# Hybrid attention and PEER layer: head-group norms in two parts, value columns moved behind the last latent head, second LayerNorm by token halves with float32 products

## The chip, the cores and the metric

The kernel runs on one core of one Trainium2 chip. The metric is device time in microseconds of one execution. The core has TensorE (PE, matmuls), VectorE (DVE), ScalarE (ACT), GpSimd (POOL, unused here) and SyncE (SP), on whose queue every DMA of this kernel is issued.

## The reference

One decoder layer on 256 tokens of width 2048, all in float32. `x` and `c` are inputs, `mod = silu(c) @ w_ada + b_ada` gives six vectors of 2048 (shift, scale and gate of the two sub-layers).

```
h   = LN0(x) * (1 + sc1) + sh1
proj = h @ w_in                       # 8 heads' q, k, v (3 x 1024), two latents of 512, a 64-wide key
o_a = dilated window attention, 8 heads of 128         # group A
o_b = latent attention (w_uq, w_uk, w_uv), 8 heads     # group B
o   = concat(rms_norm(o_a) * g_a, rms_norm(o_b) * g_b)  # each over 1024 columns
x1  = LN(alpha * x + g1 * (o @ w_o)) * ln1_g + ln1_b
h2  = LN0(x1) * (1 + sc2) + sh2
q   = h2 @ w_pq                       # scores against two key sets, top 16, softmax: gates
out = LN(alpha * x1 + g2 * (gelu(h2 @ u.T) * gates) @ v) * ln2_g + ln2_b
```

The norms need the whole row: the mean square of the 1024 columns of a head group, and mean and variance of 2048 columns.

## The kernel before

The 256 tokens stand as two halves (`th`) of 128 partitions. Activations that feed a matmul are transposed to columns: 16 chunks of 128 features by 256 tokens. Most matmuls are made in three products of a rounded part and a remainder (`mm3`, L139: hi x hi, hi x lo, lo x hi, type fp32r): `piece` (L94) loads 1 MB of weights as 4 x 512 columns, ACT rounds it to `hi` (L101), DVE takes the remainder `lo` (L103), two halves each, from rings of three `raw`, four `hi` and four `lo` buffers. Some pieces are multiplied in plain float32 (L150, L157, L334), which takes two instructions per matmul in the trace.

The stages, in order of time: w_in in four k groups (0 to about 250 us), with the products of the last group between the first heads; heads of group A 0 to 3 and of group B 0 to 7 (to 333); the norms and the last four heads of A; w_o in 16 pieces (348 to 452); the two LayerNorms in a row (`affine`, L695); w_pq in four k groups (472 to 575); the u table with the search for the top 16 (to 1320); the v table and the last LayerNorm.

Beside all of it runs the product with w_ada: `ada` (L207) loads one block of 1 MB, and DVE multiplies and sums it in two halves (L212) into one column of `modc`. 32 blocks belong to the first k groups; the other 48 (16 of the gate g1, 32 of shift and scale of the second sub-layer, in the order of the k groups that need them) come from a generator, `ada_rest` (L244), and `ada_pull(n)` (L259) asks for the next n. `PULLS`, `PULL_WO` and `PULL_PQ` say how many at which place. They go through two buffers, so that a block's load waits until DVE is done with the block two before.

A planner orders the work: it takes the instructions in the order in which the program makes them as priorities, simulates the engines, and fixes one order for each engine and for the DMA queue, in which they then run; an instruction that waits holds up all behind it on its engine. `tc.issue_after(ins)` puts the instructions of its block that are on the engine of `ins` behind it in that order.

The places that the change touches: `attend` (L415) is one head's softmax and its product with the values; a head of A reads its values from `proj` columns 2048 to 3071, which are the pieces n = 4 and 5 of w_in, the heads 4 to 7 of them piece 5 (L580). `row_norm` (L458) squares a group's 1024 columns on ACT (L462), makes the reciprocal root in small steps on DVE (`rstd_of`, L166) and scales the columns; `to_operand` (L488) transposes them (L481), scales by the gain (L485) and splits. In the program's order, the norm of B stands before heads 4 and 5 of A, and the norm of A behind the w_o pieces of steps 0 to 3, whose operands come from B alone. `spread_cols` (L229) makes the row of the gate g1 in all partitions: 16 diagonals on DVE (L235), 16 float32 matmuls against ones (L236). In `affine`, the residual's norm is applied in four pieces of 512 columns (L701, L702), with statistics of the result (L703) for the second norm (`norm_of`, L687); `to_xT` (L709) normalises, transposes (L716) and, for the first 512 columns, modulates and splits. Both halves have to be there before the first w_pq piece, since its products are 256 tokens wide.

## Time and profile before

| | us |
|---|---|
| median of 3 runs | 2043.37 (2042.28 to 2044.26) |
| profiled execution | 2044.22 |
| its span, first to last instruction | 2042.4 |
| TensorE busy | 1973.8 (97%) |
| VectorE busy | 1497.3 (73%) |
| ScalarE busy | 1048.2 (51%) |
| DMA, mean share of 16 engines | 73.5% |

A row of a timeline gives the start in us from the span's first instruction, the duration, engine, line, operation, what it writes and reads, and, in brackets, how long its engine had stood idle and what ended that. PEclk is the granted share of TensorE's full clock (2.4 GHz); it has two levels, 1.0 and 0.5. A matmul's duration holds its latency, so the distance between starts is the price of one in a row of them.

### The profile page before, as it was taken

The numbers are of one execution on the slowest core, as the hardware profiler recorded it, in microseconds if no ns is written. First come the engines' busy times: TensorE is split into PE (matmuls) and PEld (weight loads), VectorE is DVE, ScalarE is ACT, GpSimd is POOL, SyncE is SP. The second block draws the span as 40 slices with busy tenths as digits, with TensorE's granted clock in tenths as the row PEclk, the third lists the DMA queues.
The fourth block names the chain that finished last, engine by engine and source line by source line (L and its number), as shares of the span: only waits on it lengthen the run. The fifth ranks groups of instructions, "written<-read, shape, count | busy, mean of one in ns | idle before, by whom it ended". The sixth has DMA issues, their size and how long they took to land.

```text
span 2042.4 us, 26235 instructions
## 1 busy us (share of the span) xinstructions
PE 1973.8 (97%) x10072; PEld 1644.3 (81%) x10072; DVE 1497.3 (73%) x2344; ACT 1048.2 (51%) x1538; POOL 0.2 (0%) x4
## 2 busy tenths in 40 slices
PE   6999998988999999999999999999999999999997
PEld 4567686778998888888888888888888788888886
DVE  7588987889799868677777766686776666554557
ACT  2333457435444665677777775444444444444451
POOL 0000000000000000000000000000000000000000
PEclk7999998998999999999999999999999999999999
DMA  8887887867646566667777668989999988765552
GB/s 349 338 332 304 314 324 268 331 267 277 241 147 215 219 239 254 235 255 273 270 287 265 266 238 308 316 337 324 329 337 324 304 290 286 278 227 202 189 207 102
DMA packets 142830, 554.82 MB, mean 272 GB/s; under 512 B 10864, under 2 KB 77552, under 8 KB 84848
## 3 DMA queue, kind: packets, MB, share of 16 engines
q1 hardware_dynamic: 142704, 553.14, 73.5%
q8 instruction: 79, 1.29, 0.2%
q14 instruction: 47, 0.39, 0.1%
HBM read 502.76 MB, written 50.34 MB: 271 GB/s over the span
## 4 chain that ended last, share of the span: by engine, by line
PE 85%; DVE 9%; DMA 3%; ACT 2%; issue 1%; SPq 0%; DVEq 0%; ACTq 0%
PE u_ps L135 21%; PE u_ps L136 11%; PE v_ps L141 10%; PE v_ps L140 10%; PE v_ps L142 10%; PE win_ps L334 3%; DVE ada L212 2%; PE win_ps L141 2%; DMA gl<-g_d 2%; PE win_ps L142 2%; PE g_ps L942 2%; PE win_ps L140 1%; PE wo_ps L142 1%; PE wo_ps L141 1%; PE wo_ps L140 1%
## 5 line engine op out<-in xcount | busy, mean ns | idle before, releaser
L135 PE MATMUL u_ps<-act,hi_u 128*128 128x512 f32 x2048 | 721.6, 396 | 0.0
L136 PE MATMUL u_ps<-act,lo_u 128*128 128x256 f32 x2048 | 575.1, 281 | 0.9 <-DVE lo_u L103 0.9
L135 PEld LDWEIGHTS u_ps<-act,hi_u 128*128 128x128 f32 x2048 | 384.5, 188 | 87.7
L101 ACT CAST hi_v<-raw_v 128x1024 fp32r<-128x1024 f32 x244 | 256.8, 1054 | 332.0 <-PE v_ps L142 298.6
L103 DVE TENSOR_TENSOR lo_v<-raw_v,hi_v 128x1024 fp32r<-128x1024 f32 x244 | 295.6, 1222 | 173.0 <-ACT hi_v L101 172.9
L103 DVE TENSOR_TENSOR lo_u<-raw_u,hi_u 128x1024 fp32r<-128x1024 f32 x256 | 312.3, 1221 | 137.7 <-ACT hi_u L101 136.5
L136 PEld LDWEIGHTS u_ps<-act,lo_u 128*128 128x128 f32 x2048 | 386.6, 189 | 3.9 <-DVE lo_u L103 3.7
L141 PE MATMUL v_ps<-lo_v,whi 128*128 128x512 f32 x976 | 380.0, 389 | 2.3 <-DVE lo_v L103 2.3
L140 PE MATMUL v_ps<-hi_v,whi 128*128 128x512 f32 x976 | 379.9, 389 | 1.0 <-DVE W L798 1.0
L142 PE MATMUL v_ps<-hi_v,wlo 128*128 128x512 f32 x976 | 379.7, 389 | 0.0
L101 ACT CAST hi_u<-raw_u 128x1024 fp32r<-128x1024 f32 x256 | 267.3, 1048 | 174.4 <-PE u_ps L135 163.3
L141 PEld LDWEIGHTS v_ps<-lo_v,whi 128*128 128x128 f32 x976 | 183.2, 188 | 41.0 <-DVE lo_v L103 3.5
L140 PEld LDWEIGHTS v_ps<-hi_v,whi 128*128 128x128 f32 x976 | 183.2, 188 | 40.1 <-DVE W L798 1.8
L142 PEld LDWEIGHTS v_ps<-hi_v,wlo 128*128 128x128 f32 x976 | 183.2, 188 | 38.1
L212 DVE SCALAR_TENSOR_TENSOR ada<-ada,cb 128x1024 f32<-128x1024 f32 x160 | 191.0, 1218 | 9.9 <-DMA ada<-in_w_ada_dram 9.8
L937 DVE TENSOR_TENSOR o<-eq,gT 128x1024 fp32r<-128x1024 f32 x64 | 78.3, 1223 | 33.3 <-PE g_ps L942 33.3
L334 PE MATMUL win_ps<-raw_win,hmod 128*128 128x512 f32 x192 | 86.4, 605 | 1.2 <-ACT hmod L305 1.2
L799 ACT ACTIVATE W<-W 128x512 f32<-128x512 f32 x64 | 40.7, 636 | 73.4 <-DVE W L798 73.4
L140 PE MATMUL wpq_ps<-act,hi_wpq 128*128 128x256 f32 x256 | 73.6, 290 | 2.3 <-ACT act L160 2.1
L142 PE MATMUL wpq_ps<-act,lo_wpq 128*128 128x256 f32 x256 | 72.8, 286 | 0.5 <-DVE lo_wpq L103 0.5
L141 PE MATMUL wpq_ps<-act,hi_wpq 128*128 128x256 f32 x256 | 73.0, 286 | 0.0
L101 ACT CAST hi_win<-raw_win 128x1024 fp32r<-128x1024 f32 x40 | 40.9, 1049 | 61.4 <-PE win_ps L142 30.8
(329 smaller groups left out, 2407.1 us busy)
## 6 DMA issues: line engine op xcount, KB each, us to landing
raw_u<-in_u_dram SPq DMA_DIRECT2D x128, 1024.0 KB, 5.3
raw_v<-in_v_dram SPq DMA_DIRECT2D x122, 1024.0 KB, 6.6
ada<-in_w_ada_dram SPq DMA_DIRECT2D x80, 1024.0 KB, 6.9
raw_win<-in_w_in_dram SPq DMA_DIRECT2D x32, 1024.0 KB, 8.9
g_d<-stg SPq DMA_DIRECT2D x16, 2048.0 KB, 7.2
gl<-g_d SPq DMA_DIRECT2D x32, 1024.0 KB, 10.1
raw_wo<-in_w_o_dram SPq DMA_DIRECT2D x16, 1024.0 KB, 6.9
raw_wpq<-in_w_pq_dram SPq DMA_DIRECT2D x16, 1024.0 KB, 6.9
```

The costliest lines, as they stand in the source:

```text
L101: nc.scalar.copy(hi, raw[:, 2 * j:2 * j + 2, :])
L103: nc.vector.tensor_sub(lo, raw[:, 2 * j:2 * j + 2, :], hi.bitcast(F32))
L135: nc.tensor.matmul(pss[e], hi[:, i, es], act[:, k], start=first and j == 0 and i == 0, stop=False)
L136: nc.tensor.matmul(pss[e][:, 1], lo[:, i, es], act_hi[:, k, :], start=False, stop=last and j == 1 and i == 3)
L140: nc.tensor.matmul(o, sh, mh, start=start, stop=False)
L141: nc.tensor.matmul(o, sh, ml, start=False, stop=False)
L142: nc.tensor.matmul(o, sl, mh, start=False, stop=stop)
L212: nc.vector.scalar_tensor_tensor(w[:, z, :], w[:, z, :], 1.0, cb[:, z * 1024:(z + 1) * 1024], op0=ALU.mult, op1=ALU.mult, accum_out=(modc, ...
L334: nc.tensor.matmul(ps[th], act[:, i, ts], src[:, i, :], start=i == 0, stop=i == 3)
L799: nc.scalar.activation(ws, ws, AF.Gelu)
L937: nc.vector.tensor_mul(o2, eq.unsqueeze(2).broadcast_to(both), gT[:, four, :].bitcast(F32).unsqueeze(3).broadcast_to(both))
L942: nc.tensor.matmul(ps[:, q * T:(q + 1) * T], o1[:, 2 * j + q, :], o2[:, 2 * j + q].rearrange("p z n -> p (z n)"), start=True, stop=True)
```

## The change

It does the following. (1) The w_in piece n = 5 of the last k group is made behind head 7 of group B, not before the heads; the scores of heads 4 and 5 of A stand before it. (2) `row_norm` of a head group takes the squares of seven heads early (`early_squares`) and of the eighth at the end; the small steps of the reciprocal root become two fewer. (3) The norm of A and its transposes stand before the w_o pieces in the program's order; the w_ada pulls of steps 0 to 3 are queued behind `norm_done` on DVE. (4) The row of g1 is made from one transpose and one DMA to DRAM as soon as its 16 columns are there, and read back as a broadcast. (5) `affine` works in halves of 1024 columns; the second norm's sums come with the second instruction, its squares from ACT. (6) The w_pq pieces of k group 0 for n = 0, 1, 2 are multiplied in float32, one token half at a time, the first half behind the first half's norm; n = 3 remains a split piece. (7) The pulls are set anew.

```diff
-PULLS = (2, 1, 1, 3, 0, 1, 1, 1, 3, 1, 0, 1)
-PULL_WO = (2, 3, 0, 1, 1, 1, 1, 1, 0, 0, 1, 2)
+PULL_IN = (0, 1, 0)
+PULLS = (2, 1, 1, 3, 0, 1, 1, 1, 3, 1, 0, 0)
+PULL_WO = (0, 1, 1, 1, 1, 1, 1, 1, 1, 1, 1, 2)
...
-        nc.vector.tensor_mul(t, t, ve)
-        nc.vector.tensor_scalar(t, t, -0.5, 1.5, op0=ALU.mult, op1=ALU.add)
-        last_rstd[0] = nc.vector.tensor_mul(r, r, t)
+        nc.vector.scalar_tensor_tensor(t, t, -0.5, ve, op0=ALU.mult, op1=ALU.mult)
+        last_rstd[0] = nc.vector.scalar_tensor_tensor(r, t, 1.5, r, op0=ALU.add, op1=ALU.mult)
...
+    def row_of(col0):
+        ps = bank("tr", f"row_ps{col0}")
         nc.tensor.transpose(ps[:16, :P], modc[:, col0:col0 + 16], ident)
+        rowt = stream.tile([P, 2, 512], F32, tag="lo", name=f"rowt{col0}", bufs=4)[:16, 0, :P]
         nc.scalar.copy(rowt, ps[:16, :P])
         nc.sync.dma_start(row_d.rearrange("(c p) -> c p", p=P), rowt)
...
             ada_bias(G1, 16)
+            row_of(G1)
...
                         ada_in(kg + 1, m)
                         m += 1
+                    ada_pull(PULL_IN[kg])
...
+            def squares(c0, n, ms):
                 for th in range(2):
                     nc.scalar.activation(junk[:, :n], proj[:, th, c0:c0 + n], AF.Square, accum_out=ms[:, th:th + 1])
...
+            def row_norm(c0, n, name, early=None):
+                ms = mix.tile([P, 2], F32, tag="ms", name=f"ms_{name}", bufs=2)
+                if early is None:
+                    squares(c0, n, ms)
+                    nc.vector.tensor_scalar(ms, ms, 1.0 / n, 1e-6, op0=ALU.mult, op1=ALU.add)
+                else:
+                    squares(c0 + n - P, P, ms)
+                    nc.vector.scalar_tensor_tensor(ms, ms, 1.0 / n, early, op0=ALU.mult, op1=ALU.add)
...
+            def early_squares(c0, name):
+                ms = mix.tile([P, 2], F32, tag="mse", name=f"mse_{name}", bufs=1)
+                squares(c0, 1024 - P, ms)
+                nc.vector.tensor_scalar(ms, ms, 1.0 / 1024, 1e-6, op0=ALU.mult, op1=ALU.add)
+                return ms
...
-            for n in (1, 3, 5):
+            for n in (1, 3):
                 w_in_pieces(3, (n,), hmod3)
                 ada_pull(PULLS[2])
...
-            for h in (4, 5, 6, 7):
+            for h in (4, 5, 6):
                 heads_b(h)
                 ada_pull(PULLS[11])
-            row_norm(1024, 1024, "ob")
-            heads_a(2, last_a[0])
+            ms_b = early_squares(1024, "ob")
+            first[3, 5] = piece(a["w_in"][3, 5], "win3_5")
+            heads_b(7)
+            last_s = [scores_a(*last_a[0], h) for h in (4, 5)]
+            with tc.issue_after(last_o[0].ins):
+                w_in_pieces(3, (5,), hmod3)
+            row_norm(1024, 1024, "ob", ms_b)
+            heads_a(2, last_a[0], scores=last_s)
             to_operand(1024, 8, V_GOUT + 8, "ob0")
             to_operand(1536, 12, V_GOUT + 12, "ob1")
-            heads_a(3, last_a[1])
+            heads_a(3, last_a[1], (0,))
+            ms_a = early_squares(0, "oa")
+            heads_a(3, last_a[1], (1,))
+            norm_done = row_norm(0, 1024, "oa", ms_a)
+            to_operand(0, 0, V_GOUT, "oa0")
+            to_operand(512, 4, V_GOUT + 4, "oa1")
             for step in range(4):
                 w_o_piece(step)
-            norm_done = row_norm(0, 1024, "oa")
-            to_operand(0, 0, V_GOUT, "oa0")
-            to_operand(512, 4, V_GOUT + 4, "oa1")
...
-            spread_cols(g1b, modc[:, G1:G1 + KC], "g1")
+            bcast_row(g1b, row_d)
...
                 if step >= 4:
                     w_o_piece(step)
-                ada_pull(PULL_WO[step])
+                    ada_pull(PULL_WO[step])
+                else:
+                    with tc.issue_after(norm_done.ins):
+                        ada_pull(PULL_WO[step])
...
             def affine(th):
                 last_columns(th)
...
+                halves = [(r1[:, th, z * 1024:(z + 1) * 1024], slice(z * 1024, (z + 1) * 1024)) for z in range(2)]
+                for xc, cs in halves:
                     nc.vector.scalar_tensor_tensor(xc, xc, mv[:, 0:1], lng[:, cs], op0=ALU.subtract, op1=ALU.mult)
-                    nc.vector.scalar_tensor_tensor(xc, xc, r, lnb[:, cs], op0=ALU.mult, op1=ALU.add)
-                    nc.vector.bn_stats(st2[:, th, n, :], xc)
+                for z, (xc, cs) in enumerate(halves):
+                    nc.vector.scalar_tensor_tensor(xc, xc, r, lnb[:, cs], op0=ALU.mult, op1=ALU.add,
+                                                   accum_out=sums[:, 0, z:z + 1])
+                    nc.scalar.activation(sq, xc, AF.Square, accum_out=sums[:, 1, z:z + 1])
...
+                chain.append(nc.vector.tensor_scalar(nm, mq[:, 0:1], r, -1.0, op0=ALU.mult, op1=ALU.mult))
+                return r, nm
...
+            raws = [load_piece(a["w_pq"][n, 0], f"wpq{n}_0") for n in range(2)]
+            norms = [affine(th) for th in range(2)]
...
+            raws.append(spare[:, 1024:3072].rearrange("p (c n) -> p c n", c=4))
+            nc.sync.dma_start(raws[2], a["w_pq"][2, 0])
...
+            def half_piece(n, th):
+                for e in range(4):
+                    c0 = e % 2 * T + th * P
+                    for i in range(4):
+                        nc.tensor.matmul(q_ps[2 * n + e // 2][:, c0:c0 + P], raws[n][:, i, e * P:(e + 1) * P],
+                                         hq[:, i, th * P:(th + 1) * P], start=False, stop=False)
...
+            with tc.issue_after(chain[0].ins):
+                to_xT(0, *norms[0])
...
+                for n in range(3):
+                    half_piece(n, 0)
             with tc.issue_after(chain[1].ins):
+                to_xT(1, *norms[1])
+                for n in range(3):
+                    half_piece(n, 1)
+                    ada_pull(PULL_PQ[n])
...
+                w_pq_piece(3, 0)
+                to_h2(1)
+                for kg in range(1, Q_FIRST):
                     for n in range(4):
```

In the last loop, `ada_pull(100)` asks for all that is left at k group 1, n = 0, as before, and `to_h2(2)` and `to_h2(3)`, which need the last blocks, follow there.

## Rows read from the trace of the kernel before

**Rows 1.** Windows by stage: us, busy us (instructions) of each engine, granted clock, DMA.
```profile
core 0: us, PE busy (x) PEld busy (x) DVE busy (x) ACT busy (x) POOL busy (x), PEclk, DMA share, GB/s
200.00:312.00 112.00, 110.41 (x541) 82.19 (x540) 97.40 (x235) 55.31 (x122) 0.00 (x0) 1.00 0.80 310
333.00:348.00 15.00, 8.97 (x36) 6.59 (x35) 11.24 (x52) 13.35 (x28) 0.00 (x0) 0.66 0.67 251
372.00:387.00 15.00, 10.38 (x57) 8.20 (x56) 12.64 (x29) 8.52 (x15) 0.00 (x0) 0.89 0.73 265
390.00:441.00 51.00, 51.00 (x226) 42.11 (x225) 42.42 (x54) 19.97 (x20) 0.00 (x0) 1.00 0.86 345
453.00:478.00 25.00, 12.43 (x54) 10.53 (x54) 22.47 (x54) 15.58 (x31) 0.00 (x0) 0.59 0.45 171
472.00:478.00 6.00, 5.97 (x29) 5.97 (x30) 5.40 (x9) 4.55 (x8) 0.00 (x0) 0.53 0.98 382
478.00:499.00 21.00, 21.00 (x175) 20.82 (x175) 19.00 (x27) 11.14 (x13) 0.00 (x0) 1.00 0.76 295
467.00:522.00 55.00, 51.94 (x402) 51.35 (x402) 47.79 (x72) 27.40 (x39) 0.00 (x0) 0.90 0.83 322
545.00:1320.00 775.00, 774.05 (x4576) 681.67 (x4575) 586.47 (x1002) 503.80 (x839) 0.00 (x0) 1.00 0.68 250
```

**Rows 2.** Waits of TensorE, 310 to 395: us in total, times, longest us.
```profile
PE pt_a L438 <- DVE mx_a L433: 4.9, 4, 3.6
...
PE oa_ps L481 <- ACT qr_lt L485: 1.1, 1, 1.1
```

**Rows 3.** Timeline of ScalarE, 333 to 339: start us, us, line, operation.
```profile
333.75 1.05 ACT L462 ACTIVATE qr_lt<-proj 128x1024 f32<-128x1024 f32 x1
...
336.78 1.28 ACT L171 ACT_TABLE_LOAD   x1
338.07 0.20 ACT L171 ACTIVATE rs_r<-rs_ve 128x2 f32<-128x2 f32 x1
```

**Rows 4.** Groups of TensorE by line, 372 to 387: busy us, mean ns, idle before.
```profile
L236 PE MATMUL g_ps<-g_dg,ones 128*128 128x128 f32 x32 | 5.9, 343 | 2.4 <-ACT qr_lt L485 1.5 <-DVE g_dg L235 1.0
...
L481 PE MATMUL oa_ps<-ident,proj 128*128 128x128 f32 x16 | 2.3, 279 | 1.1 <-ACT qr_lt L485 1.1
```

**Rows 5.** Timeline of VectorE, norm of group a, 357 to 367.
```profile
357.29 0.17 DVE L463 TENSOR_SCALAR ms_oa<-ms_oa 128x2 f32<-128x2 f32 x1
...
366.03 0.15 DVE L177 TENSOR_TENSOR rs_r<-rs_r,rs_t 128x2 f32<-128x2 f32 x1
```

**Rows 6.** Timeline of VectorE, the two LayerNorm chains, 441 to 467.
```profile
441.26 0.69 DVE L645 TENSOR_TENSOR wo_t<-wo_ps,g1b 128x512 f32<-128x512 f32 x1 [2.37 <-PE wo_ps L142]
...
457.63 0.21 DVE L692 TENSOR_SCALAR nm_x<-mv_x,rs_r 128x1 f32<-128x1 f32 x1
...
466.88 0.21 DVE L692 TENSOR_SCALAR nm_x<-mv_x,rs_r 128x1 f32<-128x1 f32 x1
```

**Rows 7.** Timeline of TensorE, float32 products of 128 columns, 540 to 543.
```profile
540.61 1.95 PE L837 MATMUL sc_ps<-sk,qT 128*128 128x128 f32 x16
542.32 0.36 PE L140 MATMUL wpq_ps<-act,hi_wpq 128*128 128x256 f32 x1
```

**Rows 8.** Timeline of VectorE, the last w_ada half and k group 3, 517 to 525.
```profile
517.73 1.22 DVE L212 SCALAR_TENSOR_TENSOR ada<-ada,cb 128x1024 f32<-128x1024 f32 x1
...
523.58 1.22 DVE L161 TENSOR_TENSOR act<-h,act 128x1024 fp32r<-128x1024 f32 x1
```

**Rows 9.** Timeline of TensorE, the 433rd of 768 w_pq products.
```profile
529.09 0.28 PE L140 MATMUL wpq_ps<-act,hi_wpq 128*128 128x256 f32 x1
```

**Rows 10.** Groups of VectorE by line, 467 to 520.
```profile
L212 DVE SCALAR_TENSOR_TENSOR ada<-ada,cb 128x1024 f32<-128x1024 f32 x22 | 26.1, 1220 | 0.7 <-DMA ada<-in_w_ada_dram 0.7
L103 DVE TENSOR_TENSOR lo_wpq<-raw_wpq,hi_wpq 128x1024 fp32r<-128x1024 f32 x16 | 19.3, 1220 | 3.4 <-ACT hi_wpq L101 3.4
```

**Rows 11.** Group of VectorE by line, w_ada, 200 to 312.
```profile
L212 DVE SCALAR_TENSOR_TENSOR ada<-ada,cb 128x1024 f32<-128x1024 f32 x39 | 46.6, 1217 | 0.8 <-DMA ada<-in_w_ada_dram 0.8
```

More of the change, by code (lines that the diff above doesn't have):

```diff
@@ L164, in tile_hybrid_peer_block @@
     last_rstd = [None]
+    last_o = [None]
     def rstd_of(pool, var, n, eps):
@@ new lines, in affine @@
+                nc.vector.bn_aggr(mv, st1[:, th])
+                r = rstd_of(res, mv[:, 1:2], 1, 1e-5)
+                halves = [(r1[:, th, z * 1024:(z + 1) * 1024], slice(z * 1024, (z + 1) * 1024)) for z in range(2)]
+                for xc, cs in halves:
+                    nc.vector.scalar_tensor_tensor(xc, xc, mv[:, 0:1], lng[:, cs], op0=ALU.subtract, op1=ALU.mult)
+                sums = res.tile([P, 2, 2], F32, tag="sums", name=f"sums{th}", bufs=2)
+                sq = res.tile([P, 4, T], F32, tag="h2", name=f"sq{th}", bufs=1).rearrange("p a t -> p (a t)")
@@ new lines, in affine @@
+                nc.vector.tensor_scalar(mq, mq, 1.0 / D, None, op0=ALU.mult)
+                var = res.tile([P, 1], F32, tag="var", name=f"var{th}", bufs=2)
+                nc.vector.tensor_mul(var, mq[:, 0:1], mq[:, 0:1])
+                nc.vector.tensor_sub(var, mq[:, 1:2], var)
+                r = rstd_of(res, var, 1, 1e-5)
+                nm = res.tile([P, 1], F32, tag="nm", name=f"nm{th}", bufs=2)
+                chain.append(nc.vector.tensor_scalar(nm, mq[:, 0:1], r, -1.0, op0=ALU.mult, op1=ALU.mult))
@@ L733, in to_h2 @@
                 split(act_hi[:, 4 * kg:4 * kg + 4, :], act_lo[:, 4 * kg:4 * kg + 4, :], h)
-            for th in range(2):
-                _, r, nm = affine(th)
-                if th == 0:
-                    first = r, nm
+            raws = [load_piece(a["w_pq"][n, 0], f"wpq{n}_0") for n in range(2)]
+            norms = [affine(th) for th in range(2)]
+            spare = res.tile([P, 4096], F32, tag="kept1", name="spare")
+            hq = spare[:, 0:1024].rearrange("p (c t) -> p c t", c=4)
+            raws.append(spare[:, 1024:3072].rearrange("p (c n) -> p c n", c=4))
+            nc.sync.dma_start(raws[2], a["w_pq"][2, 0])
             zero = res.tile([P, 512], BF16, name="zero")
@@ L744, in cleared @@
                 nc.tensor.matmul(q_ps[j], zero[:, :P], zero, start=True, stop=False)
-            with tc.issue_after(chain[1].ins):
-                to_xT(0, *first)
-                q_ps = [bank("mm", f"wpq_ps{j}") for j in range(4)]
-                for j in range(4):
-                    cleared(j)
-            with tc.issue_after(chain[3].ins):
-                to_xT(1, r, nm)
-                q_ps += [bank(t, f"wpq_ps{4 + j}") for j, t in enumerate(("tr", "tr", "sm", "sm"))]
-                def w_pq_piece(n, kg):
-                    transposed_mm([q_ps[2 * n + e // 2][:, e % 2 * T:(e % 2 + 1) * T] for e in range(4)],
-                                  a["w_pq"][n, kg], 4 * kg, f"wpq{n}_{kg}", False,
-                                  [kg == 3 and e % 2 == 1 for e in range(4)])
-                for kg in range(Q_FIRST):
+            def half_piece(n, th):
[4 more added lines that the diff above has]
+                                         hq[:, i, th * P:(th + 1) * P], start=False, stop=False)
@@ new lines, in w_pq_piece @@
+            def w_pq_piece(n, kg):
+                transposed_mm([q_ps[2 * n + e // 2][:, e % 2 * T:(e % 2 + 1) * T] for e in range(4)],
+                              a["w_pq"][n, kg], 4 * kg, f"wpq{n}_{kg}", False,
+                              [kg == 3 and e % 2 == 1 for e in range(4)])
+            with tc.issue_after(chain[0].ins):
+                to_xT(0, *norms[0])
+                q_ps = [bank("mm", f"wpq_ps{j}") for j in range(4)]
+                q_ps += [bank("sm", f"wpq_ps{4 + j}") for j in range(2)]
+                for j in range(6):
+                    cleared(j)
+                for n in range(3):
+                    half_piece(n, 0)
@@ L761, in tile_hybrid_peer_block @@
+            with tc.issue_after(chain[1].ins):
+                to_xT(1, *norms[1])
+                for n in range(3):
+                    half_piece(n, 1)
+                    ada_pull(PULL_PQ[n])
+                q_ps += [bank("tr", f"wpq_ps{6 + j}") for j in range(2)]
+                for j in range(6, 8):
+                    cleared(j)
+                w_pq_piece(3, 0)
+                to_h2(1)
+                for kg in range(1, Q_FIRST):
                     for n in range(4):
-                        if kg == 0 and n >= 2:
-                            for j in range(2):
-                                cleared(2 * n + j)
```

65 lines of the change are left out of this document (29 added, 36 removed).

## Prediction

> **What bounds the kernel now.** After the page's busy shares, where TensorE (PE) leads, I read the windows by stage, then PE's waits in the two stages that the change touches, then the timelines there. The windows [rows 1] show where PE loses time: the late stage (545 to 1320) has PE busy for 774.05 of 775 us, and no line of the change reaches it; 390 to 441 is full too. Three short stretches are not: 333 to 348 (8.97 busy of 15), 372 to 387 (10.38 of 15) and 453 to 478 (12.43 of 25). In each the granted clock falls below 1 as well (0.66, 0.89, 0.59 on average), so that even the busy time there is partly at 1.2 GHz. Whatever the change is worth must come from these three; the columns to compare are PE busy, its count, and PEclk. The waits name what ends the idle time of the first: the softmax of the next head (pt_a, 4.9 us in four waits) [rows 2]; in the third PE waits for DVE's chain, step 4. The span is 2042.4 us, the profiled execution 2044.2, the median of the three runs 2043.4; I sum against the execution and lower the answer by the 0.8 between them.
>
> **1. Value columns held back.** The piece n = 5 of the last k group (24 products of 512 columns) moves from before the heads to the moment after head b7. One such product costs 51.0 / 226 = 0.226 us [rows 1], the piece 5.4. Where it leaves (200 to 312) PE has 110.41 of 112 us and VectorE (DVE) 97.40 [rows 1]: PE is the fuller, so 5.4 go; by DVE, which loses two casts' remainders and two additions (some 3.8), it would be 3.8. I take 5.4. Where it arrives, PE stands idle at once after head b7, 3.6 of the 4.9 us of [rows 2] in one piece, so the products fill that and cost nothing more; without this cover they would cost 5.4.
>
> **2. Norm of group b.** Squares of seven heads are taken early, so the chain keeps 128 columns instead of 1024: before, each token half takes 1.05 us [rows 3]; after it, an eighth of that and a fixed part, I estimate 0.4, 1.3 less for both. Two w_ada halves of 1.2 us that sat between the small steps leave DVE too (PULLS[11] is 0), 2.4 less. The 16 transposes of ob could then start some 3.7 us earlier, and with them the first w_o product. Head a4 now needs the held-back values, two additions after the piece. I take 3.5 for this; bounds 0 (ScalarE's exponentials and copies end last) and 5.4.
>
> By the Trainium skill (ScalarE: Activation LUTs, "What ACT_TABLE_LOAD costs") a switch of table costs a drain of 1.38 us beside the 1.28 of the load. Here the load starts at 336.78, takes 1.28, and the square root starts at 338.07 [rows 3]: no drain is to be seen. With it the two switches of this chain would leave 0.7 of the 3.5, and the sum would be 2.8 us less; the trace decides, I leave it out.
>
> **3. Norm of group a, and the row of g1.** In 372 to 387 PE needs, after the change, only the 16 transposes (2.3 us) [rows 4] and the nine w_o products there (57 instructions [rows 1] less 16 and 32, 2.0 us): the 32 products that spread g1 over the rows, 5.9 us [rows 4], and DVE's 16 diagonals are gone. 15 less 4.3 is 10.7. The condition is that the operand is there before the w_o pieces that don't need it run out. These are steps 0 to 3, 4 x 5.4 = 21.7 us. The norm took 357.29 to 366.03, 8.7 us [rows 5], most of it w_ada and w_o work of 1.2 us between dependent steps of 0.2; without w_ada (queued behind norm_done now) and with two multiplications fewer I estimate 4 to 6, and 10 more for transposes, copies and split: under 21.7. If the transposes still come last, only the 5.9 stay: bounds 5.9 and 10.7. What replaces the spreading is one transpose, one copy and 8 KB to DRAM a hundred us earlier, and a broadcast of 1 MB in the w_o stage, 3 us of DMA time at 345 GB/s; DMA has a share of 0.86 there [rows 1] and PE none idle, so I count nothing (bound 3). The w_ada block that PULL_IN brings forward lies in the projection stage beside PE work; its bound is 2.4 of DVE, I take 0.
>
> **4. Second LayerNorm.** Before, the first half's chain runs from 441.26 to the nm_x at 457.63, the second's ends at 466.88 [rows 6]. After: the affine is done in two instructions of 1024 per step instead of four of 512, and the eight statistics of the second norm leave DVE; sums come with the second affine, squares from ScalarE behind it (1.05 + 0.2 for the last half). I get the last square at 451, then ten small steps of 0.2: 453 if nothing comes between, 457 if residual and affine of the second half do, as before. I take 455.5. PE then has 32 transposes (4.6 by the 2.3 for 16), six half pieces of 16 float32 products of 128 columns, and one split piece. Eight such float32 products take 540.61 to 542.32, 0.214 each [rows 7]: 6 x 16 x 0.214 = 20.5. A split piece is 48 products of 21.0 / 175 = 0.12 [rows 1], 5.8. Together 30.9, against 4.6 + 4 x 5.8 = 27.8 before: 3.1 more work, but 10.3 of products and half the transposes no longer wait for the second half. From 456.6: 30.9, 1.5 idle, and 3 for the clock (in 472 to 478, granted 0.53, PE got 29 instructions done in 6 us that need 3.5 at 0.12 [rows 1]; I take that and a little for the transposes) end at 492.0; before, the fourth piece ended at 499.0, the end of that window. I take 7.0. Bounds: 10.5 (chain at 453), 0.7 (the whole first half at 1.2 GHz, 10.3 lost in place of 3).
>
> **5. What is late next: the w_ada stream.** Counting the pulls, 37 of 48 blocks were asked for before the LayerNorm, now 32; 16 in place of 11 stand behind the second chain, and k group 3 needs the last. Before, that operand's split is at 523.58 [rows 8], PE comes to it at 529.09, after nine pieces [rows 9]: 5.5 to spare. After, PE would come 5.4 + 3.5 + 10.7 + 7.0 = 26.6 earlier, at 502.5. The chain would end 19.6 (steps 1 to 3) and an estimated 2.9 (the statistics and shorter steps) earlier, at 444.4. From there DVE has 16 x 26.1 / 11 = 38.0 of w_ada, 12 remainders of 1.21 (three w_pq pieces need none) = 14.5, and 5 of splits: 57.5 [rows 10]. At the 0.87 busy of 467 to 522 [rows 1] that is 66, at full 57.5; I take 62, plus 4.6 from the last w_ada's end to the split [rows 8]: 511.0, 8.5 too late. So 26.6 less 8.5 = 18.1: 2044.2 - 18.1 = 2026.1, as a median 2025.
>
> **Rivals.** (a) The stream is hidden: w_pq pieces of k group 2 for other n are put in front of the late one, each 5.8 us of cover. Then all 26.6 stay: 2017. For: the pieces are independent; against: before, n = 0 was finished first. (b) The transposes of oa hold PE up. They now stand before the w_o pieces; if the planned order has them earlier than the norm allows, all w_o products behind them wait. Before, PE stood 1.1 us at such a transpose with w_o products behind it [rows 2]. It costs step 2 (3.5) and the 4.8 between step 3's bounds; the chain shifts along, so 18.1 - 8.3 = 9.8: 2034. The Trainium skill (TensorE: Matmul & The Clock Gate, "Step-by-step: what each phase is for") says that matmuls stay in program order and only weight loads are pulled ahead; by that rule such a wait is not stepped over, and the trace agrees with its 1.1. (c) Slower: the w_ada stream keeps the pace of 200 to 312, 39 halves in 112 us, 5.7 per block [rows 11]. 16 x 5.7 = 91 from 444.4, plus 4.6: 540.0 against 529.1, 10.9 slower, 2054. It decides from 5.0 per block on ((529.1 - 4.6 - 444.4) / 16); in 467 to 520 it was 53 / 11 = 4.8 [rows 10], not far off. Against it: DVE has fewer remainders between the blocks, and fewer transfers share the queue. (d) The planner's order stays as it was, and the gaps with it: 2043.
>
> **How the numbers follow.** Forecast 0.50, (a) 0.18, (b) 0.18, (c) 0.08, (d) 0.06. Range 2013 to 2038: it leaves out (c) and (d) and holds (a) and (b) with a few us for the bounds of steps 2 to 4. A change of 0.2% (4 us) is about what a measurement of this kernel tells from none: faster 0.86, same 0.06, slower 0.08.
>
> **What would show it.** The first idle stretch after head b7 gone and win_ps products in its place (1); first w_o product some 9 us earlier (1, 2); no g_ps products and the w_o products without a break from the first to the last columns, which end some 20 us earlier (3); float32 wpq_ps products of 128 columns before the second nm, 96 in all with two records each (4); PE idle of about 8 us before the k group 3 pieces, and w_ada blocks 16 behind the chain (5). Wrong, if w_o products break off for want of lo_wo, if the idle before k group 3 is over 20 or under 3 us, or if the clock stays low through the half pieces.

## The result, and the profile after

The changed kernel takes 2057.2 us (2053.6 to 2059.0, 5 runs) against 2044.3 us; the ratio is 1.0059 [1.0044, 1.0074]. It is slower by 13 us; 2025 was forecast. The profiled execution took 2058.5 us, its span is 2056.8, 14.4 more than before.

Four points at which TensorE (PE) changes its work are read first, and the kernels are compared by them all through. Start of the k group 3 of w_in (first kr_ps product): 196.0 before, 215.7 after, **19.7 later**. First w_o product: 348.1 and 362.8, 14.7 later, so the heads gain 5.0. Last w_o product: 451.8 and 471.5, 19.7 later, so the w_o stage **loses** 5.0. Last w_pq product: 574.9 and 589.6, 14.7 later, so the LayerNorm and w_pq gain 5.0. From there on both take the same 1467 us. For the first point, the group of kr_ps products, before and then after (durations, first and last start):

```profile
L310 PE MATMUL kr_ps<-kw,hmod x16: 218/275/275, 196.0 to 198.1; 128*128 128x64 f32 x16
```
```profile
L315 PE MATMUL kr_ps<-kw,hmod x16: 217/275/275, 215.7 to 217.3; 128*128 128x64 f32 x16
```

The first loss lies ahead of all four main edits (steps 1 to 4 of the prediction). The windows (columns as in [rows 1]), before and then after:

```profile
110.00:140.00 30.00, 28.32 (x117) 21.49 (x116) 29.29 (x45) 11.92 (x13) 0.00 (x0) 1.00 0.98 399
340.00:372.00 32.00, 30.60 (x139) 24.33 (x139) 28.31 (x74) 24.03 (x42) 0.00 (x0) 0.88 0.68 256
```
```profile
110.00:140.00 30.00, 22.41 (x74) 15.99 (x73) 24.52 (x40) 7.04 (x9) 0.00 (x0) 0.83 0.76 306
140.00:216.00 76.00, 65.88 (x248) 46.38 (x247) 63.99 (x104) 21.13 (x25) 0.00 (x0) 0.96 0.88 361
340.00:372.00 32.00, 28.02 (x154) 21.88 (x153) 15.55 (x66) 27.95 (x68) 0.00 (x0) 0.95 0.12 44
400.00:455.00 55.00, 46.93 (x181) 35.85 (x181) 47.15 (x70) 15.97 (x16) 0.00 (x0) 0.91 0.88 359
472.00:488.00 16.00, 8.65 (x45) 7.88 (x45) 13.61 (x41) 9.29 (x20) 0.00 (x0) 0.68 0.53 213
```

In 110 to 140 PE falls from 28.32 to 22.41 us, and the granted clock from 1.00 to 0.83. Before, VectorE (DVE) was busy there for 29.29 of 30 us and DMA at 0.98: no room for more in these 30 us. PE's waits from 110 to the k group 3, before and after (us, times, longest), name the remainders of the w_in weights:

```profile
PE win_ps L141 <- DVE lo_win L103: 4.5, 2, 3.0
```
```profile
PE win_ps L142 <- DVE lo_win L104: 15.5, 8, 3.0
PE win_ps L141 <- ACT hi_win L102: 2.0, 3, 1.3
```

SP's waits in the same stretches: a w_ada load that waits for DVE to empty one of its buffers stands at the queue's head for 14.3 us before, 51.4 after.

```profile
SPq L210 <- DVE ada L212: 14.3, 3, 6.2
```
```profile
SPq L214 <- DVE ada L216: 51.4, 9, 9.9
```

The timeline of SP shows what went in: two w_ada loads between every two w_in loads, where before the two alternated. Before, and then after:

```profile
116.53 0.33 SPq L85 DMA_DIRECT2D raw_win<-in_w_in_dram  x1
116.91 0.43 SPq L210 DMA_DIRECT2D ada<-in_w_ada_dram  x1
117.39 0.43 SPq L85 DMA_DIRECT2D raw_win<-in_w_in_dram  x1
117.86 0.47 SPq L210 DMA_DIRECT2D ada<-in_w_ada_dram  x1
```
```profile
111.62 9.65 SPq L214 DMA_DIRECT2D ada<-in_w_ada_dram  x2
121.36 0.38 SPq L86 DMA_DIRECT2D raw_win<-in_w_in_dram  x1
126.11 6.99 SPq L214 DMA_DIRECT2D ada<-in_w_ada_dram  x2
133.19 0.38 SPq L86 DMA_DIRECT2D raw_win<-in_w_in_dram  x1
```

`ada_pull(PULL_IN[kg])` stands inside the loop over the column groups, and the k group 1 has six of them: six blocks are pulled, not one. So 37 blocks are asked for ahead of the LayerNorm and 11 behind it, as before, not 32 and 16.

The second loss begins at 340: DMA has a share of 0.12 until 372, where before it had 0.68 (windows above). SP issues three loads between 337 and 382, and a w_ada load only then, when the norm of group a is done (378.5):

```profile
336.83 0.42 SPq L868 DMA_DIRECT2D iota<-in_consts_dram  x1
361.50 20.32 SPq L86 DMA_DIRECT2D raw_wo<-in_w_o_dram  x3
382.63 0.33 SPq L214 DMA_DIRECT2D ada<-in_w_ada_dram  x1
```

At the head of SP's queue stand w_o loads in these us, which wait until VectorE is done with earlier w_o pieces (SP's waits, 300 to 460, after; the last number is the longest):

```profile
SPq L86 <- DVE lo_wo L104: 30.1, 2, 24.2
SPq L86 <- DVE ms_oa L475: 13.3, 1, 13.3
```

What is missing between them are the w_ada loads: the products that would empty their two buffers are held, and the first of them starts at 378.44.

```profile
378.44 1.22 DVE L216 SCALAR_TENSOR_TENSOR ada<-ada,cb 128x1024 f32<-128x1024 f32 x1
```

What was not moved then is missing in 400 to 455: PE does 46.93 of 55 us at a clock of 0.91. Before, 390 to 441 was full [rows 1]. PE's waits in 400 to 480 after:

```profile
PE h_ps L758 <- ACT xc L755: 6.1, 1, 6.1
PE wo_ps L142 <- DVE lo_wo L104: 3.9, 2, 2.1
PE wpq_ps L791 <- DVE wo_t L677: 2.2, 2, 1.7
PE wo_ps L142 <- DVE kept L162: 2.0, 1, 2.0
```

The other rows of before, as they are after: the wait at pt_a [rows 2] is 0.4 us; the last squares of group b [rows 3] take 0.32, then come the table and the root, but the squares of the seven other heads run only just ahead of them (347.91 and 349.09), behind head b7's last product (348.0); oa's transposes stand among w_o products without a wait, and there are no g_ps products [rows 4]; the norm of group a [rows 5] takes 375.04 to 378.5; the two nm [rows 6] come at 477.7 and 485.6, the half pieces [rows 7] behind them; the 22 w_ada halves behind the chain [rows 10] take 25.9 us.

```profile
349.09 0.95 ACT L464 ACTIVATE qr_lt<-proj 128x896 f32<-128x896 f32 x1
...
350.86 0.31 ACT L464 ACTIVATE qr_lt<-proj 128x128 f32<-128x128 f32 x1
...
351.68 1.28 ACT L176 ACT_TABLE_LOAD   x1
352.98 0.20 ACT L176 ACTIVATE rs_r<-ms_ob 128x2 f32<-128x2 f32 x1
```
```profile
L500 PE MATMUL oa_ps<-ident,proj 128*128 128x128 f32 x16 | 2.3, 278 | 0.2
```
```profile
375.04 0.15 DVE L475 SCALAR_TENSOR_TENSOR ms_oa<-ms_oa,mse_oa 128x2 f32<-128x2 f32 x1
...
378.36 0.16 DVE L181 SCALAR_TENSOR_TENSOR rs_r<-rs_t,rs_r 128x2 f32<-128x2 f32 x1
```
```profile
L746 DVE TENSOR_SCALAR nm<-mv_x,rs_r x2: 206/210/215, 477.7 to 485.6; 128x1 f32<-128x1 f32 x2
```
```profile
L216 DVE SCALAR_TENSOR_TENSOR ada<-ada,cb 128x1024 f32<-128x1024 f32 x22 | 25.9, 1217 | 0.4 <-DMA ada<-in_w_ada_dram 0.4
```

### The profile page after: what moved, and what is told of

Same layout as the page of the kernel before. It is cut to its first block, busy times and chain, and to the rows that moved or that the text cites. A ratio compares the mean times of both kernels' runs of the same rounds, so it can differ in the third digit from the quotient of the medians.

```text
span 2056.8 us, 26207 instructions
## 1 busy us (share of the span) xinstructions
PE 1979.5 (96%) x10088; PEld 1645.7 (80%) x10089; DVE 1484.3 (72%) x2304; ACT 1041.9 (51%) x1541; POOL 0.2 (0%) x4
## 4 chain that ended last, share of the span: by engine, by line
PE 86%; DVE 8%; DMA 3%; ACT 2%; issue 1%; SPq 0%; DVEq 0%; ACTq 0%
PE u_ps L136 21%; PE u_ps L137 11%; PE v_ps L142 10%; PE v_ps L143 10%; PE v_ps L141 10%; PE win_ps L339 3%; DMA gl<-g_d 2%; PE win_ps L142 2%; PE win_ps L143 2%; DVE ada L216 2%; PE g_ps L1003 1%; PE wo_ps L142 1%; PE wo_ps L143 1%; PE win_ps L141 1%; PE wo_ps L141 1%
## 5 line engine op out<-in xcount | busy, mean ns | idle before, releaser
L142 PE MATMUL win_ps<-lo_win,act 128*128 128x512 f32 x160 | 67.6, 423 | 16.8 <-DVE lo_win L104 16.6
L339 PEld LDWEIGHTS win_ps<-raw_win,hmod 128*128 128x128 f32 x192 | 37.4, 198 | 45.1 <-issue 42.6
L1006 ACT COPY stg<-g_ps 128x512 f32<-128x512 f32 x128 | 72.2, 624 | 0.0
```

The source lines that it names most:

```text
L142: nc.tensor.matmul(o, sh, ml, start=False, stop=False)
L339: nc.tensor.matmul(ps[th], act[:, i, ts], src[:, i, :], start=i == 0, stop=i == 3)
L1006: nc.scalar.copy(stg[:, :, :, t:t + 2], ps.rearrange("p (t z i) -> p z i t", t=2, z=2))
```

## The experiments

All in one table: median; ratio to the kernel before with its interval; then from the profiled execution the start of k group 3 and how long each stage took after it (heads: to the first w_o product; w_o: to the end of the last; w_pq: from there to the end of the last w_pq product), in us. Kernels with the same early code start k group 3 between 191 and 197, so a difference of up to 6 us at that point tells nothing in one profile. The ratio is to the kernel before as measured beside each kernel (2044.3 to 2047.5 us), so kernels of different rows are best compared by it. The profiled executions of e10 (2041.8 us), e14 (2036.2) and e17 (2032.2) lie 5 to 7 us from their medians.

| kernel | median | ratio | k group 3 | heads | w_o | w_pq |
|---|---|---|---|---|---|---|
| before | 2044.3 | | 196.0 | 152.1 | 103.7 | 123.1 |
| after | 2057.2 | 1.0059 [1.0044, 1.0074] | 215.7 | 147.1 | 108.7 | 118.1 |
| e1 | 2064.3 | 1.0098 [1.0071, 1.0124] | 215.0 | 152.4 | 104.6 | 120.8 |
| e2 | 2053.1 | 1.0035 [1.0024, 1.0045] | 195.2 | 146.4 | 106.5 | 138.1 |
| e3 | 2045.7 | 1.0004 [0.9990, 1.0019] | 215.6 | 151.6 | 93.6 | 114.9 |
| e4 | 2036.2 | 0.9955 [0.9937, 0.9974] | 196.4 | 147.3 | 106.7 | 117.4 |
| e5 | 2060.6 | 1.0068 [1.0046, 1.0089] | 216.2 | 146.8 | 107.7 | 117.9 |
| e6 | 2040.9 | 0.9978 [0.9966, 0.9990] | 212.8 | 150.9 | 93.6 | 117.3 |
| e7 | 2043.4 | 0.9991 [0.9980, 1.0002] | 195.6 | 153.9 | 100.6 | 125.9 |
| e8 | 2033.7 | 0.9943 [0.9925, 0.9961] | 194.8 | 152.1 | 104.0 | 115.0 |
| e9 | 2050.2 | 1.0014 [1.0003, 1.0025] | 208.0 | 147.3 | 107.1 | 117.7 |
| e10 | 2047.8 | 1.0007 [0.9995, 1.0020] | 203.3 | 147.1 | 107.6 | 118.1 |
| e11 | 2056.1 | 1.0030 [1.0009, 1.0052] | 201.4 | 160.0 | 102.5 | 119.8 |
| e12 | 2059.9 | 1.0070 [1.0047, 1.0093] | 200.8 | 165.1 | 103.2 | 120.3 |
| e13 | 2039.4 | 0.9970 [0.9957, 0.9983] | 192.7 | 150.5 | 108.6 | 116.7 |
| e14 | 2043.5 | 0.9990 [0.9978, 1.0001] | 191.0 | 150.5 | 107.3 | 120.0 |
| e15 | 2036.5 | 0.9947 [0.9927, 0.9967] | 193.5 | 147.2 | 102.3 | 123.7 |
| e16 | 2035.1 | 0.9948 [0.9931, 0.9966] | 194.9 | 150.5 | 104.2 | 116.9 |
| e17 | 2027.5 | 0.9899 [0.9879, 0.9920] | 196.7 | 156.3 | 95.5 | 112.5 |
| e18 | 2048.4 | 1.0010 [0.9999, 1.0020] | 195.6 | 157.4 | 102.5 | 120.1 |

**e1: the early blocks alone, on the kernel before.**
```diff
+PULL_IN = (0, 1, 0)
...
                         m += 1
+                    ada_pull(PULL_IN[kg])
```


> The kernel before, with the one line of the change that pulls w_ada blocks in the second k group of the w_in stage, and nothing else of it. The line stands inside the loop over six column groups, so it pulls six blocks of 1 MB, not one. Theory A (the six blocks are the loss: on SP's queue each waits for one of two buffers, and the w_in weights behind it wait too): k group 3 starts near 214 to 216 us instead of 196, and of these 18 to 20 us a few come back later because six fewer blocks stand behind the LayerNorm: 2057 (2053 to 2063). Rival A0 (the early loss comes from another edit): k group 3 stays at 196 and the time is 2044 or, with fewer blocks later, 2040.

k group 3 starts at 215.0, and the kernel is 18.7 us slower: one line makes the whole early loss. Theory A holds; of the "few us later" only 2.3 come back (w_pq), and the time is just above its range.

**e2: the change without them.**
```diff
-PULL_IN = (0, 1, 0)
+PULL_IN = (0, 0, 0)
```


> The changed kernel without the six early blocks; they now come last, so that 17 instead of 11 stand behind the second LayerNorm chain. Theory A: k group 3 starts near 196 again (19.7 us gained), and the longer stream gives 0 to 12 of it back before the operand of the last k group: 2044 (2037 to 2050). Rival A0: the early loss stays, and the longer stream adds to it: 2057 to 2069.

k group 3 is back at 195.2, as theory A has it, but only 4 of the 20 us stay, and the time is 3 us above its range: w_pq takes 138.1 us instead of 118.1. The products of the last of 17 blocks end at 538.9, the rounded part of the operand of the k group 3 of w_pq is ready at 543.3, and PE begins the group at once. This is step 5 of the forecast, with 17 blocks for its 16. Ahead of it PE also stands 12.3 us from 520.6 on, for the weights of another piece (hi_wpq), whose load is issued only at 522.3, behind two w_ada loads, and the granted clock is 0.61 from 533 to 540.

**e3: the hold taken away.**
```diff
-                else:
-                    with tc.issue_after(norm_done.ins):
-                        ada_pull(PULL_WO[step])
+                ada_pull(PULL_WO[step])
```


> The changed kernel with the w_ada blocks of the first four w_o steps no longer held behind the norm of group a. Theory B (held back, they leave the DMA engines idle from 340 to 372 us, and the megabytes that were not moved then are missing at 405 to 447, where PE stands for lo_wo and its clock falls): the breaks of PE in the w_o products go, 6 us of idle and some 5 of lower clock; the early loss stays: 2047 (2043 to 2052). Rival B1 (the w_o stage is bound by its own weights and the rows of x, g1 and the LayerNorm, whatever the order): 2057. Rival B2 (the blocks delay the norm of group a on VectorE, and the products wait for its operand): 2060.

It gains 11.5 us, and w_o falls from 108.7 to 93.6. DMA between 340 and 372 has 0.61 (after: 0.12):

```profile
340.00:372.00 32.00, 26.12 (x134) 20.33 (x134) 24.67 (x81) 24.65 (x62) 0.00 (x0) 0.89 0.61 230
```

Between 339 and 376 seven w_ada loads are issued here, after none; between the w_o loads at 338.55 and 364.97 SP issues no other w_o load here either. Theory B holds; B1 and B2 fall.

**e4: e3 with the blocks pulled nearly as before.**
```diff
-PULL_IN = (0, 1, 0)
+PULL_IN = (0, 0, 0)
-PULLS = (2, 1, 1, 3, 0, 1, 1, 1, 3, 1, 0, 0)
-PULL_WO = (0, 1, 1, 1, 1, 1, 1, 1, 1, 1, 1, 2)
+PULLS = (2, 1, 1, 3, 0, 1, 1, 1, 3, 1, 0, 1)
+PULL_WO = (2, 3, 1, 1, 1, 1, 1, 1, 0, 1, 1, 2)
```


> The changed kernel with the w_ada blocks pulled nearly where the kernel before pulls them: none in the w_in stage, two and three at the first w_o steps, not held back; 13 stand behind the second chain. Theories A and B together: both losses go, 19.7 and some 9, and the longer stream gives back up to 3: 2030 (2024 to 2036), which would be what the four main edits are worth. Rival C (the main edits bring less than forecast, and only the early loss was in the way): 2038 to 2043.

Faster than before, by 9 us, but not by the 14 expected: w_o is back at 106.7. Neither theory nor rival C alone: something else takes what the edits save there.

**e5: the early loads on GpSimd's queue** (on the changed kernel).
```diff
-        nc.sync.dma_start(w, a["w_ada"][j].rearrange("p (z n) -> p z n", z=2))
+        queue[0].dma_start(w, a["w_ada"][j].rearrange("p (z n) -> p z n", z=2))
...
+                    queue[0] = nc.gpsimd
                     ada_pull(PULL_IN[kg])
+                    queue[0] = nc.sync
```


> The changed kernel with the loads of the six early w_ada blocks issued from GpSimd's queue instead of SP's; same bytes, same two buffers, same work on VectorE, the hold behind the norm of group a kept. Theory A1 (the loss of 19.7 us is the waiting in SP's queue: a w_ada load that waits for a buffer keeps the w_in weights behind it from being issued): 13 to 18 us come back, k group 3 starts at 198 to 203, 2042 (2038 to 2045). Rival A2 (the loss is the 6 MB and the 14 us of VectorE in a stage that has neither to spare, or the two buffers themselves): k group 3 starts at 212 to 216, 2055 to 2057.

Nothing comes back (216.2). In 110 to 160 the loads now flow (DMA 0.99; after: 0.86), and PE still does 36.02 us (after: 36.72):

```profile
110.00:160.00 50.00, 36.02 (x124) 25.25 (x123) 43.75 (x66) 12.09 (x12) 2.11 (x4) 0.90 0.99 393
```

My theory A1, that the waits in SP's queue are the cost, falls; rival A2 stands, at a time 4 us above its range. (The page lists GpSimd's queue as another kind, software_dynamic; a second queue of SP's kind wasn't tried.)

**e6: the six blocks in k group 0** (on e3).
```diff
-PULL_IN = (0, 1, 0)
+PULL_IN = (1, 0, 0)
```


> The changed kernel without the hold behind the norm of group a (as in e3), and with the six early blocks pulled in the first k group of the w_in stage instead of the second, on SP's queue. In 60 to 110 us the kernel before has a DMA share of 0.74 and VectorE busy for 29.6 of 50 us, in 110 to 140 it has 0.98 and 29.3 of 30. Theory A3 (what the six blocks cost depends on the room in the stage where they are put): they cost 0 to 6 us there, and of the 2045.7 of e3 13 to 19 go: 2029 (2026 to 2034). Rival A1 in its strict form (any w_ada block that stands between the w_in loads in SP's queue holds them up by the wait for a buffer, wherever): k group 3 starts after 210, 2043 to 2046.

k group 3 starts at 212.8: 17 of the 19.7 us are lost there too. A3 falls: by the ratios the kernel is 5 us faster than e3, not 13 to 19. The blocks went in earlier than the window of the expectation: from 47 us on two w_ada loads stand ahead of a w_in load. Before, DMA had 0.95 from 40 to 60 and 0.86 from 60 to 85, and VectorE was busy for 71.0 of the 100 us from 40 to 140. So the window with DMA at 0.74 was not what was tried, and what sets the price in k group 0 stays open.

**e7: the row of g1 alone; e8: the second LayerNorm alone** (on the kernel before).
```diff
             ada_bias(G1, 16)
+            row_of(G1)
-            spread_cols(g1b, modc[:, G1:G1 + KC], "g1")
+            bcast_row(g1b, row_d)
```


> The kernel before with only the row of g1 changed: one transpose, a copy and 8 KB to DRAM after the last g1 block, and a broadcast of 1 MB in the w_o stage, in place of 16 diagonals on VectorE and 32 products on TensorE. By the forecast the 5.9 us of products go and nothing is given back: 2038 (2036 to 2040). Rival D1 (the w_o stage is bound by its transfers, so the broadcast's MB costs about 3 of them): 2041. Rival D2 (the w_o stage waits for its weights anyway): 2044.

2.1 us and not sure to be any; the forecast falls, and D1 and D2 are not told apart. w_o is 3.2 shorter, w_pq 2.8 longer: PE's first transpose (h_ps) comes 11.6 us behind the last w_o product, before 6.9, with a wait of 5.6 for wo_t that wasn't there.

```diff
-                    nc.vector.bn_stats(st2[:, th, n, :], xc)
...
+                    nc.scalar.activation(sq, xc, AF.Square, accum_out=sums[:, 1, z:z + 1])
...
+                for n in range(3):
+                    half_piece(n, 0)
```


> The kernel before with only the second LayerNorm of the change: affine in halves of 1024, sums and squares in place of the statistics, six float32 half pieces. By the forecast it is worth 7.0 us (0.7 to 10.5): 2037 (2034 to 2042). In e3 the stretch from the last w_o product to the last w_pq product is 8.2 us shorter than before, in e4 5.7 and in the changed kernel 5.0. Rival E1 (it gains only where the w_o stage ends late for another reason, and the w_ada stream behind the chain takes the rest): under 3 us, 2042 to 2045.

11.9 us by the medians, 8.1 of them in the w_pq stretch; more than the 7.0 forecast. **It beats both kernels, and nothing that I ran on the whole computation beats it** (e15 and e16 are level with it). PE waits 2.1 us for the first transposes, which come 3.9 us behind the last w_o product (before 6.9, after 7.3), and the clock is at half from 455.8 to 459.2, where before it was from 457.2 to 477.7.

**e9 and e10: half the bytes, or an eighth of the products,** of the six early blocks (on the changed kernel).
```diff
+        if early[0]:                                      # e9
+            nc.sync.dma_start(w[:, 0, :], wide[:, 0, :])
...
+            nc.vector.scalar_tensor_tensor(w[:, z, :], w[:, 0 if early[0] else z, :], 1.0,
...
+            m = 128 if early[0] else 1024                 # e10
+            nc.vector.scalar_tensor_tensor(w[:, z, :m], w[:, z, :m], 1.0, cb[:, z * 1024:z * 1024 + m], op0=ALU.mult,
```


> The changed kernel, in which the six early w_ada blocks load only their first half (0.5 MB each) and both products on VectorE read that half; the second half of these blocks is left out of the sum. Same places, buffers and work on VectorE. Theory A4 (the w_in stage is bound by its transfers, and the six blocks cost what their bytes cost): half of the 19.7 us comes back, k group 3 starts at 206 (203 to 209), 2047. Rival A5 (VectorE's 14 us, which lie in front of the remainders lo_win that TensorE waits for): k group 3 stays at 213 to 216, 2055 to 2058.

> The changed kernel, in which the six early w_ada blocks are loaded whole, but their products on VectorE take only 128 of each 1024 columns; the rest of these sums is left out. 12 products of 1.22 us become some 0.3, 11 us less on VectorE. Theory A4 (transfers): k group 3 stays at 213 to 216, 2055 to 2058. Rival A5 (VectorE): it starts at 203 to 206, 2045 to 2048. If both e9 and this one give part back, the two loads add up: the loads wait for a buffer that VectorE has to empty.

Start of k group 3, e9 and then e10:

```profile
L321 PE MATMUL kr_ps<-kw,hmod x16: 218/275/275, 208.0 to 209.6; 128*128 128x64 f32 x16
```
```profile
L318 PE MATMUL kr_ps<-kw,hmod x16: 217/275/275, 203.3 to 204.9; 128*128 128x64 f32 x16
```

Half the bytes give back 7.7 of 19.7 us, seven eighths of the products 12.4; by the ratios of the whole times 9 and 11 of the 13. Neither A4 nor A5 alone, but the last case of e10's expectation: both loads cost. In the changed kernel neither is full from 110 to 215 (DMA 0.85, VectorE busy for 88.18 of 105 us; before, 0.89 and 76.08 of 86 from 110 to 196): PE waits 15.5 us for VectorE's remainders, and VectorE, which runs in a fixed order, 10.8 for PE's sums.

**e11 and e12: all later w_ada loads on GpSimd's queue,** on e4 and e8.
```diff
             hmod3 = group_start(3)
+            queue[0] = nc.gpsimd
```


> e4 (the changed kernel with the w_ada blocks pulled as before) with all w_ada loads from the heads on issued from GpSimd's queue instead of SP's. In e4 SP waits 51 us in 300 to 460 with a w_ada load at its head, while w_o weights stand behind it, and TensorE breaks off six times in the w_o products for 8.2 us in all, with 6.8 us of lower clock. Theory F (SP's queue holds the w_o weights up): these breaks go, 2028 (2025 to 2032). Rival G (as e5 showed for the w_in stage, the queue is not the limit: a w_ada load that no longer waits only goes ahead of weights): 2035 to 2040.

> e8 (the kernel before with the second LayerNorm alone) with all w_ada loads from the heads on issued from GpSimd's queue. Its w_o products wait for the norm of group a and the spreading of g1, not for weights. Theory F: SP's queue costs it little, 2031 to 2034. Rival G: w_ada loads go ahead of weights, 2036 to 2040.

20 and 26 us slower than e4 and e8 by the medians, 15 and 26 by the ratios: theory F falls, and rival G has the direction at several times its price. The loss lies in the heads, which grow to 160 and 165 us, and k group 3 comes 5 to 6 us late; what lengthens the heads wasn't tried. e11's w_o is 4.2 shorter than e4's, so what SP's queue costs in that stage alone stays open. The loads of 170 to 215 in e4 and then in e11 (KB each, median us from issue to landing):

```profile
raw_win<-in_w_in_dram SPq DMA_DIRECT2D x6, 1024.0 KB, 11.7
ada<-in_w_ada_dram SPq DMA_DIRECT2D x6, 1024.0 KB, 9.7
```
```profile
raw_win<-in_w_in_dram SPq DMA_DIRECT2D x6, 1024.0 KB, 13.9
ada<-in_w_ada_dram POOLq DMA_DIRECT2D x4, 1024.0 KB, 8.1
```

Out of SP's queue the w_ada loads land sooner there, and the weights later.

**e13 to e16: parts put together.** e13 is e8 and the head edits; e14 adds the early squares of group a; e15 and e16 are e4 with these lines:
```diff
+PULL_WO = (1, 1, 1, 1, 1, 1, 1, 1, 1, 1, 1, 2)                          # e15
...
-            row_of(G1)                                                    # e16
...
-            bcast_row(g1b, row_d)
+            spread_cols(g1b, modc[:, G1:G1 + KC], "g1")
```


> The kernel before with the second LayerNorm and the head edits (held-back value columns, early squares of group b, early scores of a4 and a5); the norm of group a, its transposes and the spreading of g1 stay where they were, and the w_ada blocks nearly too. Theory H (these two parts are worth what they showed, the LayerNorm 11.9 us in e8, the heads the 4.4 by which e4 reaches the first w_o product earlier): 2029 (2026 to 2033). Rival I (the w_o stage is bound by its loads, so that what it gains by starting earlier it gives back as waits for weights): 2033 to 2036.

> e13 with the early squares of group a as well; the four w_o pieces still stand ahead of its norm, and g1 is spread as before. Theory H: the operand of group a comes some 2 us earlier, and the idle of 2.8 us around its transposes goes: 2027 (2024 to 2031). Rival I: as e13.

> e4 with one w_ada block at each of the first four w_o steps instead of 2, 3, 1 and 1, and one more at two later ones; 15 blocks instead of 13 stand behind the second LayerNorm chain. Theory J (in e4 these blocks stand ahead of the w_o weights in a stage bound by loads): 3 to 6 of the 8 us of breaks go, 2032 (2029 to 2035). Rival K (what leaves the w_o stage is missing behind the LayerNorm, as with the 17 blocks of e2, where TensorE stood 12.3 us): 2036 to 2042.

> e4 with the spreading of g1 as before: 32 products and 16 diagonals in place of the broadcast of 1 MB. Theory I (the w_o stage is bound by its loads: 5.9 us of products that need no weights cost it little, and 1 MB less is loaded): 2034 to 2038, like e4. Rival L (TensorE's work sets the stage): 2042.

e13 and e14 are no faster than e8 but slower (e14's runs scatter from 2036 to 2048): theory H falls. Rival I has the direction, but its 2033 to 2036 is passed by 3.4 and 7.5 us; why stays open. e16 puts 5.9 us of products back and loses nothing, as I says. e15 shortens w_o by 4.4 and finds 6.3 more in w_pq: rival K. In the profiled executions of e4, e8 and e13 to e16 the last w_pq product ends at 567.8, 565.8, 568.4, 568.8, 566.7 and 566.5, whatever the w_o stage did.

**e17 and e18: the control.** Half of each w_ada block from the heads on, in e4 and in the kernel before.
```diff
             hmod3 = group_start(3)
+            half[0] = True      # load w[:, 0, :] only, both products read it
```


> e4 (all four main edits, w_ada blocks pulled nearly as before), in which every w_ada block from the heads on loads only its first half and both products read that half; the second half of these blocks is left out of the sums. Work on VectorE, buffers and places are the same; some 20 MB less is loaded between 200 and 566 us. Theory I (the loads set the pace there, and so the four edits give back what they save): the breaks of TensorE in the w_o products and before the LayerNorm shrink, 2036 becomes 2026 (2021 to 2031), and the distance to the kernel before with the same halving is 15 us or more. Rival M (VectorE's work or the dependencies set the pace): 2033 to 2037, and the distance stays near 9.

> The kernel before with the same halving of the w_ada blocks from the heads on, as the control of e17; the second half of these blocks is left out of the sums. Theory I: TensorE stands there for the softmax, the norms and the spreading of g1, hardly for loads, so the halving gives at most 4 us: 2042 (2040 to 2046). Rival M: as much as in e17, whatever that is.

With the loads light, the four edits are worth 20.8 us by the medians (2048.4 to 2027.5), 15.0 by the spans. The kernel before gains nothing by the same relief, 2 us above theory I's range: its w_o and w_pq are 1.2 and 3.0 us shorter, but its heads 5.3 longer. In e17 against e4 w_o and w_pq are 11.2 and 4.9 shorter, the heads 9.0 longer. Why halved loads lengthen the heads wasn't tried; the two later stages are what the control compares. The w_o stage in e4, then in e17 and in e18:

```profile
360.00:460.00 100.00, 85.16 (x359) 66.58 (x357) 83.61 (x132) 36.81 (x49) 0.00 (x0) 0.94 0.83 333
```
```profile
360.00:460.00 100.00, 96.40 (x464) 78.33 (x463) 81.97 (x140) 51.28 (x75) 0.00 (x0) 1.00 0.70 270
```
```profile
360.00:460.00 100.00, 91.86 (x423) 74.04 (x421) 76.34 (x131) 45.50 (x58) 0.00 (x0) 1.00 0.61 227
```

PE does 85.16 us of the 100 in e4 and 96.40 in e17, with the same work on VectorE (83.61 and 81.97). For w_o theory I holds and M falls.

## Why the prediction was wrong

**The step that failed** is the last sentence of step 3: "The w_ada block that PULL_IN brings forward lies in the projection stage beside PE work; its bound is 2.4 of DVE, I take 0." It fails twice. The line stands in a loop and pulls six blocks, and alone it makes the early loss (e1). And a block costs 3.3 us there on average (19.7 / 6), not 0 to 2.4: I bounded it by DVE's time alone, and both its bytes and its products cost (e9, e10). No row of the forecast looked at that stage; the window 110 to 140 would have shown it full.

**Step 1 and step 2**, 8.9 together, of which 5.0 came. Step 1 was right: the idle behind head b7 is gone, the held-back products stand in it, and from the first kr_ps product to head b7's last one it takes 132.4 us, before 137.2: 4.8 for the 5.4. (As much in e4, but only 0.3 to 1.6 in e3, e6, e13, e14 and e16, where PE breaks off for 2 us and more in all among the last heads of b; what sets the one or the other wasn't tried.) Step 2 brought nothing, its lower bound: from there to the first w_o product it takes 14.7 us, before 14.9. The early squares run behind head b7, so the root comes 5.0 us behind its last product, before 4.9. And the root isn't what the first w_o product waits for: in e3 it comes 2.7 us behind, and the stretch is 14.8. No drain shows around the table load here either: load to 352.96, root at 352.98. So the Trainium skill's 1.38 us (ScalarE: Activation LUTs, "What ACT_TABLE_LOAD costs") is again not seen.

**Step 3**, 10.7: the size was right and the cover wrong. Where the loads are far enough ahead (e3, e6) w_o takes 93.6 us, 10.1 less than before. In the changed kernel it takes 108.7, because I took the hold ("queued behind norm_done now") as a gain alone: I counted what it spares DVE, and not that the w_ada loads, whose buffers the held products keep, stop with them, so that DMA falls to a share of 0.12 for 32 us. That cost 11.5 (e3). And with the pulls nearly as before (e4) the loads hold w_o up, and most of the 10 us come back when they are halved (e17: 95.5, against 106.7 in e4 and 102.5 in e18).

**Step 4**, 7.0: the stretch is 5.0 shorter after, 8.1 alone (e8), 7.7 in e17 against e18. After, the first transpose comes 7.3 us behind the last w_o product, in e8 3.9; the forecast's 456.6 is 4.8 behind the 451.8 of before. The first half's chain starts later against that product (8.2 us ahead of its end, before and in e8 10.5), and the second half's residual and first affine stand between its last small steps, the case for which I had 457 and not 455.5:

```profile
471.54 0.69 DVE L677 TENSOR_TENSOR wo_t<-wo_ps,g1b 128x512 f32<-128x512 f32 x1 [0.19 <-PE wo_ps L143]
...
475.29 1.28 DVE L729 SCALAR_TENSOR_TENSOR r<-r,mv_r,lng 128x1024 f32<-128x1024 f32 x1
...
477.68 0.21 DVE L746 TENSOR_SCALAR nm<-mv_x,rs_r 128x1 f32<-128x1 f32 x1
```

**Step 5**, 8.5 given back: by the same miscount not due, as 11 blocks stand behind the chain. As a mechanism it holds: 13 blocks leave no idle for the operand of the k group 3 (e4), 15 some 3.2 us (e15), and 17 delay it to 543.3, with 12.3 us of idle for weights just ahead (e2).

Of the signs of being wrong two came: w_o products break off for lo_wo (3.9 us), and there is no idle ahead of the k group 3 of w_pq. Of the rivals none came true: (b)'s wait of oa's transposes is 0.2 us, and (c)'s time is near 2057 for another reason. So 18.1 forecast against 14.4 lost by the spans: 19.7 for the early blocks, 15.7 that w_o lost against the forecast (+5.0 for -10.7), 3.9 less from the heads, less 6.5 in the last stretch (-5.0 for +1.5), 32.8 in all; 0.3 of rounding and later stages remain.

## What to carry to other kernels

Count a call by the loop that it stands in, and price what it adds in the stage where it lands, by both its bytes and its engine's time; here a block of 1 MB and 2.4 us of VectorE cost 3.3 us on average in a stage that began with DMA at 0.98 and VectorE at 29.3 of 30 us, and some 2.8 in the k group before it (e6). A wait put on an engine's work also stops the loads that need its buffers: look at the DMA share of the next stretch before you call it free. When several edits shorten TensorE's work in a stage that loads hold up, a second may pay nothing (e8 alone 11.9 us, all four edits in e4 9): lighten the loads and time both kernels again, to see what is hidden.
